# A feed-forward product whose moving operand and whose sums are walked backwards in time

## The chip, the core and the metric

The kernel runs on one core of a Trainium2 chip. The metric is the device time of one execution in microseconds (us), the median over several runs. A smaller time is better. A core has a matrix engine (PE in the profile: matmuls; PEld: the loads of its weights), a vector engine (DVE), an activation engine (ACT), a general engine (POOL), and a queue for transfers (SP). PE reads its operands from the on-chip memory and writes its sums to a separate accumulator memory, PSUM, in banks of 128 rows by 512 fp32 numbers.

## The reference, cut to what matters

The whole block is a token mixing (two attention branches, gates, an output projection, a layer norm) and then a gated feed-forward. The change touches only the first product of the feed-forward, `x @ w_ffn_in`.

```python
x = layer_norm(DEEPNORM_ALPHA * x + merged @ w_out[layer], ln1_g[layer], ln1_b[layer])
u, g = jnp.split(x @ w_ffn_in[layer], 2, axis=-1)
h = jax.nn.gelu(causal_dwconv(u, conv_w[layer], conv_b[layer])) * g
x = layer_norm(DEEPNORM_ALPHA * x + h @ w_ffn_out[layer], ln2_g[layer], ln2_b[layer])
```

There are 512 frames, 1024 channels, and 2816 hidden channels for each of `u` and `g`. All numbers are fp32.

## The kernel before

The feed-forward works on transposed data: channels lie on the 128 rows of the memory, and frames run along each row. After the first layer norm the tile `x1h` holds the 8 blocks of 128 channels by 512 frames, rounded to the short fp32 format that PE takes, and `x1l` holds what the rounding left over. Every weight piece comes the same way, as a rounded part (`whi`) and a rest (`wlo`), which ACT (L104) and DVE (L113) make from what a transfer brought.

`ffn_in` (L932 to L939) computes one block of 128 hidden channels for a range of frames `c`. It runs over the 8 blocks of input channels, and for each issues three products into the same PSUM bank: rounded by rounded (L937), weight by rest (L938), weight's rest by rounded (L939). So one block takes 24 products that add up in place. The weights are the stationary operand; the frames are the moving operand, which is streamed column by column, and column t of the sum lands in column t of the bank.

The call sites are in the main body. The first three blocks (`u0`, `g0`, `u1`) are done in two halves of 256 frames, `t_lo` and `t_hi` (L1036 to L1041), because the last quarter of the frames is turned between them. All other blocks take the 512 frames at once (`full`): `g1` at L1044, and then in the loop over f from 2 to 21 `u{f}` at L1059 and `g{f}` at L1074. Together these are 44 blocks: 41 of 24 products with 512 frames, and 3 of 48 products with 256.

When the bank of `u` is full, ACT copies it to a padded tile (L980), DVE runs the causal convolution of width 3 over it (L982 to L984), ACT applies the GELU (L985), and DVE multiplies it with the bank of `g` (L993). Between the blocks PE also issues the products of the feed-forward's second matrix that are ready (`first_products`, L1024 to L1029, through `product`, L1013 to L1019). For f = 2 these open two new banks P0 and P1.

The order of the instructions on each engine is fixed when the program is built; at run time an engine takes its instructions in that order and waits on semaphores. PSUM has two banks for `u` and `g` in the loop, so the reader of a bank has the length of a block or more to empty it.

Of the kernel before, what the change touches and what calls it, by code (L numbers as in the profile page):

```python
# [23 lines left out]
KC = D // 128  # L24
# [103 lines left out]
def tile_block(ctx: ExitStack, tc: tile.TileContext, xT, xN, w_qi, w_ki, w_t, w_v, w_br, w_o, w_fi, w_fo,  # L128
               bg, cw, rel, onehot, lnp, out):
    nc = tc.nc  # L130
# [25 lines left out]
    def pa(name):  # L156
        return psA.tile([128, 512], F32, tag="A", name=name)

    def pb(name):
        return psB.tile([128, 512], F32, tag="B", name=name)  # L160
# [47 lines left out]
    ps = pb("idle_ps")  # L208
# [91 lines left out]
    for k in range(KC):  # L300
# [8 lines left out]
        wh, wl = st.get(f"qi{k}")  # L309
        for n in range(4):  # L310
            c = slice(n * 128, n * 128 + 128)
# [360 lines left out]
    for a, b in ((0, 512), (512, NREL)):  # L672
        ps = pa("line_ps")
# [134 lines left out]
    for p in range(4):  # L808
        wh_wl = st.get(f"ba{p}")
        for n in (2 * p, 2 * p + 1):  # L810
            if n not in early and n not in gps:
                gps[n] = whole(proj_t(f"ga{n}"))
            ps = pb("ba_ps")
            wh, wl = wh_wl
            for k in range(4):
                c = slice((n % 2) * 512 + k * 128, (n % 2) * 512 + k * 128 + 128)
# [39 lines left out]
    x1h = qp.tile([128, KC, S], F32R, name="x1h")  # L856
    x1l = qp.tile([128, KC, S], F32R, name="x1l")
# [74 lines left out]

    def ffn_in(w, ps, c):
        wh, wl = w
        for k in range(KC):
            kc = slice(k * 128, k * 128 + 128)
            nc.tensor.matmul(ps[:, c], wh[:, kc], x1h[:, k, c], start=(k == 0), stop=False)  # L937
            nc.tensor.matmul(ps[:, c], wh[:, kc], x1l[:, k, c], start=False, stop=False)  # L938
            nc.tensor.matmul(ps[:, c], wl[:, kc], x1h[:, k, c], start=False, stop=(k == KC - 1))  # L939

# [93 lines left out]
    for w, ps in zip(w0, ps0):  # L1036
        if ps is ps0[2]:
            turn(NB - 1)
        ffn_in(w, ps, t_lo)
    for w, ps in zip(w0, ps0):  # L1040
        ffn_in(w, ps, t_hi)  # L1041
    activate(0, ps0[0], ps0[1])
    g1_ps = pa("g_ps")
    ffn_in(st.get("g1"), g1_ps, full)  # L1044
    activate(1, ps0[2], g1_ps)
    close(ac)
# [252 lines left out]
```

## Time and profile before

| what | value |
|---|---|
| time, median of 3 runs | 746.79 us (746.69 to 747.53) |
| span of the profiled execution, first to last instruction | 744.9 us |
| the profiled execution's own time | not listed apart from the three runs; they lie 1.8 to 2.6 us above its span |
| PE busy | 735.6 us, 99% of the span |
| DVE, ACT, POOL busy | 572.0, 408.0, 148.8 us |
| PE's granted clock | 0.998 of full speed over the span |

The profile is one execution, recorded instruction by instruction. A row of a timeline gives the start in us, the length in us, the engine, the line of the kernel, the operation with its tiles (output, then inputs), and the shape. The length of a matmul runs from its first column to its modelled end, and the next one starts before that end, so the price of a matmul in a dense run is the distance from start to start and not its length.

### The profile page before, as it was taken

What the parts mean: (1) busy time and instruction counts of PE and PEld (TensorE: products, weight loads), DVE (VectorE), ACT (ScalarE), POOL (GpSimd) and SP (SyncE); (2) the same over time, 40 slices, a digit from 0 to 9 for tenths busy, and PEclk for the clock granted to TensorE, in tenths of its full rate; (3) what the DMA queues carried; (4) which work ended last, traced back from release to release, by engine and by line L of the source; (5) the groups of instructions that cost most, each with busy time, mean ns of one, the idle gap of its engine ahead of it and who ended that gap; (6) DMA issues with size and microseconds to landing.
All of it is one profiled execution on the core that took longest, in us unless ns stands there. A gap on an engine that the chain in (4) does not pass through costs nothing.

```text
span 744.9 us, 9755 instructions
## 1 busy us (share of the span) xinstructions
PE 735.6 (99%) x3477; PEld 616.9 (83%) x3477; DVE 572.0 (77%) x907; ACT 408.0 (55%) x572; POOL 148.8 (20%) x161
## 2 busy tenths in 40 slices
PE   9999999999999999999999999999999999999995
PEld 7888888888888888888889888888888888888885
DVE  5569888999679898668755866686767668668985
ACT  6466867797785587845473533443444344345430
POOL 0002224365743332000101111011101101110011
PEclk9999999999999999999999999999999999999999
DMA  7445887796476455527832544444443444448632
GB/s 266 157 128 188 207 172 173 158 214 163 116 181 154 135 126 136 131 85 247 289 57 86 170 141 142 141 143 143 141 166 114 161 136 149 144 140 268 202 130 84
DMA packets 73631, 117.03 MB, mean 157 GB/s; under 512 B 42536, under 2 KB 42792, under 8 KB 73584
## 3 DMA queue, kind: packets, MB, share of 16 engines
q1 hardware_dynamic: 66304, 93.98, 42.0%
q0 software_dynamic: 5744, 18.38, 9.9%
q10 hardware_dynamic: 1536, 4.06, 2.1%
q8 instruction: 27, 0.44, 0.3%
q14 instruction: 20, 0.16, 0.1%
HBM read 95.93 MB, written 9.98 MB: 142 GB/s over the span
## 4 chain that ended last, share of the span: by engine, by line
PE 89%; DVE 3%; POOL 2%; issue 2%; DMA 2%; ACT 2%; DVEq 0%; POOLq 0%; ACTq 0%
PE u_ps L937 5%; PE u_ps L939 5%; PE g_ps L937 5%; PE u_ps L938 5%; PE g_ps L939 5%; PE g_ps L938 5%; PE m L1019 2%; PE m L1017 2%; PE m L1018 2%; PE av_ps L511 2%; PE ga_ps L234 2%; PE ga_ps L233 2%; PE gb_ps L235 2%; PE gb_ps L234 2%; PE ga_ps L235 2%; PE gb_ps L233 2%
## 5 line engine op out<-in xcount | busy, mean ns | idle before, releaser
L104 ACT ACTIVATE whi<-raw 128x1024 fp32r<-128x1024 f32 (+1 forms) x124 | 123.8, 1001 | 143.1 <-PE g_ps L938 43.7
L113 DVE TENSOR_TENSOR wlo<-raw,whi 128x1024 fp32r<-128x1024 f32 (+1 forms) x105 | 123.9, 1181 | 36.3 <-ACT whi L104 35.6
L939 PE MATMUL u_ps<-x1h,wlo 128*128 128x512 f32 (+1 forms) x192 | 71.4, 372 | 0.0
L937 PE MATMUL u_ps<-x1h,whi 128*128 128x512 f32 (+1 forms) x192 | 71.3, 372 | 0.0
L938 PE MATMUL u_ps<-x1l,whi 128*128 128x512 f32 (+1 forms) x192 | 71.3, 371 | 0.0
L937 PE MATMUL g_ps<-x1h,whi 128*128 128x512 f32 (+1 forms) x184 | 69.9, 380 | 0.0
L938 PE MATMUL g_ps<-x1l,whi 128*128 128x512 f32 (+1 forms) x184 | 69.9, 380 | 0.0
L939 PE MATMUL g_ps<-x1h,wlo 128*128 128x512 f32 (+1 forms) x184 | 69.9, 380 | 0.0
L939 PEld LDWEIGHTS u_ps<-x1h,wlo 128*128 128x128 f32 x192 | 36.2, 188 | 6.3
L938 PEld LDWEIGHTS u_ps<-x1l,whi 128*128 128x128 f32 x192 | 36.2, 188 | 6.3
L937 PEld LDWEIGHTS u_ps<-x1h,whi 128*128 128x128 f32 x192 | 36.2, 188 | 6.2
L939 PEld LDWEIGHTS g_ps<-x1h,wlo 128*128 128x128 f32 x184 | 34.6, 188 | 6.6
L938 PEld LDWEIGHTS g_ps<-x1l,whi 128*128 128x128 f32 x184 | 34.6, 188 | 6.5
L937 PEld LDWEIGHTS g_ps<-x1h,whi 128*128 128x128 f32 x184 | 34.6, 188 | 6.5
L960 DVE TENSOR_TENSOR t<-raw 128x512 f32<-128x512 f32 x11 | 7.6, 693 | 40.1 <-DMA raw<-in_w_fo_dram 39.2
L569 POOL TENSOR_TENSOR bm<-win,score 128x256 f32<-128x256 f32 (+2 forms) x24 | 26.9, 1147 | 32.2 <-DMA pl<-bm 27.3
L985 ACT ACTIVATE c<-c,cwt 128x512 f32<-128x512 f32 x22 | 15.9, 725 | 27.5 <-DVE c L984 27.3
L979 POOL MEMSET u<- 128x2 f32 x22 | 2.1, 98 | 143.7 <-ACT whi L104 99.2
L993 DVE TENSOR_TENSOR hF<-g_ps,c 128x512 f32<-128x512 f32 x22 | 15.1, 687 | 19.7 <-PE g_ps L939 19.7
L835 POOL TENSOR_TENSOR rstd<-rstd,mhalf 128x1 f32<-128x1 f32 x8 | 7.7, 959 | 104.6 <-DVE rstd L834 104.6
L423 DVE MAX8 m<-score 128x8 f32<-128x256 f32 (+2 forms) x48 | 26.6, 556 | 0.9
L557 POOL TENSOR_TENSOR beta<-beta,keep 128x1280 f32<-128x1280 f32 x8 | 21.6, 2704 | 26.7 <-DVE keep L554 26.7
(576 smaller groups left out, 2088.3 us busy)
## 6 DMA issues: line engine op xcount, KB each, us to landing
raw<-in_w_fi_dram SPq DMA_DIRECT2D x44, 512.0 KB, 3.3
raw<-in_w_t_dram SPq DMA_DIRECT2D x32, 512.0 KB, 3.7
raw<-in_w_fo_dram SPq DMA_DIRECT2D x26, 512.0 KB, 4.2
wlo<-in_w_t_dram POOLq DMA_DIRECT2D x14, 512.0 KB, 5.8
raw<-in_w_br_dram SPq DMA_DIRECT2D x8, 512.0 KB, 4.0
raw<-in_w_o_dram SPq DMA_DIRECT2D x8, 512.0 KB, 4.1
raw<-in_w_v_dram SPq DMA_DIRECT2D x7, 512.0 KB, 4.6
raw_b<-in_w_fo_dram SPq DMA_DIRECT2D x6, 512.0 KB, 5.5
```

What stands on the lines that cost most here:

```text
L104: self.high = nc.scalar.activation(hi[:, :w], t[:, :w], AF.Copy).ins
L113: self.done[key] = eng.tensor_sub(lo[:, :w], t[:, :w], r32(hi[:, :w])).ins
L233: nc.tensor.matmul(ps[:M], wh[:, c], xh[k], start=(k == 0), stop=False)
L234: nc.tensor.matmul(ps[:M], wh[:, c], xl[k], start=False, stop=False)
L235: nc.tensor.matmul(ps[:M], wl[:, c], xh[k], start=False, stop=(k == KC - 1))
L423: nc.vector.max(m8, sc)
L557: nc.gpsimd.tensor_mul(beta, beta, keep[:, 1:ATT + 1])
L569: nc.gpsimd.tensor_add(bm[:, OFF[j]:OFF[j] + N], win[:, 512 - N:512], score[j])
L937: nc.tensor.matmul(ps[:, c], wh[:, kc], x1h[:, k, c], start=(k == 0), stop=False)
L938: nc.tensor.matmul(ps[:, c], wh[:, kc], x1l[:, k, c], start=False, stop=False)
L939: nc.tensor.matmul(ps[:, c], wl[:, kc], x1h[:, k, c], start=False, stop=(k == KC - 1))
L985: nc.scalar.activation(c, c, AF.Gelu_apprx_tanh, bias=cwt[:, f, 3:4])
```

## The change

Both the moving operand and the output of the three products get a step of -1 along the frames. The last frame of the range is streamed first, and its sum goes to the last column of the range, so that column t of the bank still holds frame t.

```diff
     def ffn_in(w, ps, c):
         wh, wl = w
+        dst = ps[:, c][:, ::-1]
         for k in range(KC):
             kc = slice(k * 128, k * 128 + 128)
-            nc.tensor.matmul(ps[:, c], wh[:, kc], x1h[:, k, c], start=(k == 0), stop=False)
-            nc.tensor.matmul(ps[:, c], wh[:, kc], x1l[:, k, c], start=False, stop=False)
-            nc.tensor.matmul(ps[:, c], wl[:, kc], x1h[:, k, c], start=False, stop=(k == KC - 1))
+            xkh, xkl = x1h[:, k, c][:, ::-1], x1l[:, k, c][:, ::-1]
+            nc.tensor.matmul(dst, wh[:, kc], xkh, start=(k == 0), stop=False)
+            nc.tensor.matmul(dst, wh[:, kc], xkl, start=False, stop=False)
+            nc.tensor.matmul(dst, wl[:, kc], xkh, start=False, stop=(k == KC - 1))
```

Two lines are added, so L937, L938 and L939 become L939, L940 and L941, and everything behind them moves down by two. In the built program every one of these products has a step of -1 and starts at the last element of its range, on the read side and on the write side. The stationary operand is as before. No instruction stands elsewhere on any engine, and the waits are the same but for one: the first product into bank P1 (for f = 2) now also waits for a semaphore of PE itself, at the count which the last product of `g1` sets. PE gets one more instruction for it, a bare semaphore wait, since a product carries one wait.

## The prediction

> **What bounds the kernel now.** I read the page's head and its first part, then the chain that ended last, then PE's waits, to learn whether a longer matmul could hide anywhere.
>
> ```profile
> span 744.9 us, 9755 instructions
> ...
> PE 735.6 (99%) x3477; PEld 616.9 (83%) x3477; DVE 572.0 (77%) x907; ACT 408.0 (55%) x572; POOL 148.8 (20%) x161
> ...
> PE 89%; DVE 3%; POOL 2%; issue 2%; DMA 2%; ACT 2%; DVEq 0%; POOLq 0%; ACTq 0%
> ```
>
> PE is busy for 735.6 of 744.9 us, and 89% of the chain that ended last is PE. A busy PE need not be at its peak, so the next view is who PE waited for; its columns are the total wait, the number of waits and the longest, in us.
>
> ```profile
> PE idle_ps L210 <- DVE idle L207: 1.2, 1, 1.2
> PE bs_ps L613 <- DVE wlo L113: 0.3, 1, 0.3
> PE qi_ps L312 <- ACT whi L104: 0.3, 1, 0.3
> ```
>
> These three are all, and none is in the feed-forward. Then the busy time by stretches: the half-width blocks (390.6 to 407), the full blocks (407 to 673), and the tail.
>
> ```profile
> 390.60:407.00 16.40, 16.40 (x138) 16.36 (x137) 8.67 (x14) 6.49 (x8) 2.18 (x5) 1.00 0.22 66
> 407.00:673.00 266.00, 266.00 (x1183) 220.60 (x1182) 191.10 (x253) 109.76 (x138) 35.91 (x53) 1.00 0.44 147
> 673.00:744.90 71.90, 64.38 (x315) 54.40 (x313) 58.39 (x87) 24.86 (x28) 6.02 (x8) 0.97 0.51 169
> ```
>
> The columns are the stretch and its length, then PE, PEld, DVE, ACT and POOL busy, the granted clock, and transfers. In the feed-forward's main stretch PE has no gap at all (266.00 of 266.00) at the full clock, while DVE is busy for 191.10 and ACT for 109.76. So the first product sits on the path with every nanosecond, and the others have room: **whatever one product gains or loses goes into the time in full**.
>
> How much of the span do the touched products hold? Their groups, of one shape each (busy us, mean ns of one, idle before), and two pairs from the timeline:
>
> ```profile
> L937 PE MATMUL g_ps<-x1h,whi 128*128 128x512 f32 x168 | 65.4, 389 | 0.0
> L937 PE MATMUL u_ps<-x1h,whi 128*128 128x512 f32 x160 | 62.2, 389 | 0.0
> ...
> L937 PE MATMUL u_ps<-x1h,whi 128*128 128x256 f32 x32 | 9.1, 285 | 0.0
> ...
> L937 PE MATMUL g_ps<-x1h,whi 128*128 128x256 f32 x16 | 4.5, 283 | 0.0
> ```
> ```profile
> 559.92 0.39 PE L937 MATMUL u_ps<-x1h,whi 128*128 128x512 f32 x1
> ...
> 565.36 0.39 PE L937 MATMUL g_ps<-x1h,whi 128*128 128x512 f32 x1
> ```
> ```profile
> 407.74 0.28 PE L939 MATMUL u_ps<-x1h,wlo 128*128 128x256 f32 x1
> ...
> 408.94 0.40 PE L937 MATMUL g_ps<-x1h,whi 128*128 128x512 f32 x1
> ```
>
> L938 and L939 have the same counts as L937, so there are 3 x (168 + 160) = 984 products of 512 frames and 3 x (32 + 16) = 144 of 256. From 559.92 to 565.36 stand 24 products, one every 226.7 ns; from 407.74 to 408.94 stand 10 of the narrow ones, one every 120 ns. Together 984 x 0.2267 + 144 x 0.120 = 223.1 + 17.3 = **240.4 us**, a third of the span. The two distances give the price of a frame as well: (226.7 - 120) / 256 = 0.417 ns, and a fixed part of 226.7 - 512 x 0.417 = 13.3 ns.
>
> **The change, part by part.** It moves no instruction, removes none, and adds one bare wait. There are three terms: the price of a frame when the stream runs backwards, the fixed part of a product, and the wait.
>
> *The frame.* 984 x 512 + 144 x 256 = 540,672 frames are streamed at 0.417 ns. No matmul of this profile has a step of -1, so the price is bounded by the nearest rows. On the low side stand matmuls whose moving operand is not one run: the attention's weighted sum reads 384 columns as three runs of 128 that lie 384 apart, beside 384 adjacent columns in the indexer's product.
>
> ```profile
> L314 PE MATMUL qi_ps<-xh,wlo 128*128 128x384 f32 x32 | 9.4, 335 | 0.0
> ...
> L511 PE MATMUL av_ps<-ptl,va 128*128 128x384 f32 x16 | 5.4, 336 | 0.0
> ```
>
> 336 against 335 ns: leaving a run costs nothing that can be seen. But these are two hops in 384 columns on the read side alone, and the sums go to adjacent columns in both. On the high side stands the only work here that steps by -1, a running product on DVE that reads two operands and writes one backwards (L554), against DVE's forward work on two operands (means over 11 of each).
>
> ```profile
> 80.98 1.21 DVE L554 TENSOR_TENSOR_SCAN keep<-keep,first 128x512 f32<-128x512 f32 x1
> ...
> 83.98 0.67 DVE L554 TENSOR_TENSOR_SCAN keep<-keep,first 128x256 f32<-128x256 f32 x1
> ```
> ```profile
> L962 DVE TENSOR_TENSOR raw<-raw,raw 128x512 f32<-128x512 f32 x11 | 7.5, 682 | 0.1
> ...
> L1000 DVE TENSOR_TENSOR hF<-hF 128x256 f32<-128x256 f32 x11 | 4.6, 419 | 0.0
> ```
>
> Backwards, an element costs (1.21 - 0.67) / 256 = 2.1 ns; forwards (682 - 419) / 256 = 1.03 ns. The factor of two may be the direction, or that each element of a running product needs the one before it; these rows can't part the two. I take it as the upper bound: one frame in two clocks, 0.833 ns, so 540,672 x 0.417 = +225 us. Below nothing I see no room: each frame must still pass, and 0.42 ns is also what lies between L314's 384 columns and L937's 512, (389 - 335) / 128. Between ends so far apart I take the matmul rows, since they are of the same engine and show that it forms an address for each column and isn't held to one ascending run: **0 us**. The step has the same size as before, and two frames that follow each other are still neighbours, on both sides. The upper end is kept for the range.
>
> *The fixed part.* 13.3 ns of each product aren't streaming. The first address is the far end of the same row. If turning cost as much again it would be 1128 x 13.3 = +15 us, and if all of it went, -15 us; nothing in the change touches it, and I take 0.
>
> *The wait.* The first product into P1 now waits for the end of the last product of `g1`, and a bare semaphore instruction comes before it. In the trace before:
>
> ```profile
> 414.18 0.39 PE L939 MATMUL g_ps<-x1h,wlo 128*128 128x512 f32 x1
> ...
> 420.52 0.39 PE L1017 MATMUL P<-whi,ah 128*128 128x512 f32 x1
> ```
>
> The one ends at 414.57, the other starts at 420.52: the condition has held for 6 us when it is asked. What such an instruction costs is seen where PE already has one, in the same stage:
>
> ```profile
> L937 PEldq EVENT_SEMAPHORE  x1: 51/51/51, 663.3 to 663.3; - x1
> ```
> ```profile
> 663.06 0.39 PE L939 MATMUL u_ps<-x1h,wlo 128*128 128x512 f32 x1
> 663.28 0.39 PE L937 MATMUL u_ps<-x1h,whi 128*128 128x512 f32 x1
> 663.51 0.39 PE L938 MATMUL u_ps<-x1l,whi 128*128 128x512 f32 x1
> ```
>
> It takes 51 ns in PE's sequencer, and the products around it keep their distance (0.22, 0.23 us), since the sequencer is ahead of the array. So 0; without that cover, 0.05 us. Behind it on PE stands all of the feed-forward, but 0.05 us once is nothing here.
>
> *The readers.* Column t of a bank still holds frame t, and ACT's copy and DVE's product wait for the last of the 24 products as before. They see no difference. If PE were slower they would only wait longer.
>
> **The sum.** 744.9 + 0 + 0 + 0 = 744.9 us of span. The three timed runs lie 1.8 to 2.6 us above the profiled span, their median 1.9 us; with that the forecast is **746.8 us**, the median of before.
>
> **The rivals.** *One frame in two clocks (slower).* PE takes 0.417 ns a frame, the fastest rate it shows. If that rate needs two frames to be fetched or stored as one ascending pair, a step of -1 splits each pair. It decides as soon as either side, the read or the sums, has this condition. 540,672 x 0.417 = +225 us gives 972 us, or 957 us if the 13.3 ns then hide behind the slower stream (512 x 0.833 = 427 instead of 226.7 ns: 984 x 0.200 + 144 x 0.093 = 210). For it speaks the factor of two on DVE; against it the runs of L511, which only bear on reading.
> [...]
>
> *A part of it.* Say one clock is lost in every fourth frame: 540,672 / 4 x 0.417 = +56 us, 803 us. No row has such a price; it stands for all that lies between 762 and 957.
>
> *A price at the turn.* Up to 13.3 ns more for each product, at most +15 us: up to 762 us. Against it: the L511 products start at many places of their rows and show no such thing.
>
> *The change doesn't do what it says.* Were the direction dropped on the way to the chip, the time would be that of the forecast, but the built instructions hold the step of -1, so this is no case of its own.
>
> **How the numbers follow.** No cost 0.62; a price at the turn 0.06; a part 0.06; one frame in two clocks 0.22; worse than that 0.03; a gain from the fixed part 0.01. The forecast's own range is 745.5 to 748.2 us, 0.2% to either side (about what a measurement of this kernel can tell from no change). That holds only 0.62, and turn and part together raise it to 0.74, so a range that holds 8 in 10 must reach the two-clock case: 745.5 to 975 us. Faster 0.01, within 0.2% 0.62, slower 0.37.
>
> **What would show it.** In the profile after, one product of 512 frames should start every 227 ns and one of 256 every 120 ns. A distance near 427 to 440 ns and 213 to 227 ns is the two-clock rival; the same surplus on both widths is a price at the turn; a surplus in the ratio of the widths is a price of the frame. P1's first product should follow P0's last by 0.23 us. If PE's distances stay and the time still moves, my reading that nothing else changes is wrong. The forecast fails if the chip pairs frames by an ascending step rather than by where they lie.

## The result, and the profile after

The changed kernel takes 754.29 us (median of 4 runs, 753.66 to 754.48) against 747.16 us before in the same comparison: a ratio of 1.0095, 95% interval 1.008 to 1.011. It is slower by 7.1 us. The head of the page, its first part and the chain by engine:

```profile
span 752.3 us, 9756 instructions
...
PE 742.8 (99%) x3477; PEld 617.1 (82%) x3477; DVE 571.8 (76%) x907; ACT 408.7 (54%) x572; POOL 149.5 (20%) x161
...
PE 89%; DVE 4%; POOL 2%; issue 2%; ACT 1%; DMA 1%; SPq 0%; DVEq 0%; POOLq 0%; ACTq 0%
```

PE is busy for 7.2 us more; the other engines' busy times are within 1 us of what they were. By stretches (length, then busy time of PE, PEld, DVE, ACT, POOL, granted clock, transfers), cut where the same work begins and ends:

```profile
407.80:680.70 272.90, 272.90 (x1184) 221.00 (x1183) 191.12 (x253) 110.02 (x138) 35.84 (x53) 1.00 0.43 143
680.70:752.30 71.60, 64.13 (x314) 54.20 (x312) 58.40 (x87) 24.54 (x27) 6.03 (x8) 0.97 0.49 169
```

The full blocks again leave PE no gap and the clock is full, but they last 272.9 us for the same work (to one product at the cut) instead of 266.0. So each product takes longer. Two pairs from the timeline, 24 products of 512 frames apart and 15 of 256 apart:

```profile
559.51 0.40 PE L939 MATMUL g_ps<-x1h,whi 128*128 128x512 f32 x1
...
565.11 0.40 PE L939 MATMUL u_ps<-x1h,whi 128*128 128x512 f32 x1
```
```profile
407.83 0.28 PE L939 MATMUL u_ps<-x1h,whi 128*128 128x256 f32 x1
...
409.61 0.40 PE L939 MATMUL g_ps<-x1h,whi 128*128 128x512 f32 x1
```

A product of 512 frames starts every 5.60 / 24 = **233.3 ns instead of 226.7**; one of 256 frames every 1.78 / 15 = **118.7 ns instead of 120**. Summed over all start-to-start distances of the touched products, the 984 wide ones take 229.6 us after 223.1 (+6.6), the 144 narrow ones 17.2 after 17.4 (-0.2). Products that stand between them take 0.2 us more. That is 6.6 of the 7.4 us of span. The rest, 0.9 us, lies ahead of the feed-forward, whose first product starts at 391.7 instead of 390.8 us. Most of it is there long before a changed product runs: a bare wait of PE that starts at 28.55 us before starts at 29.28 after. In the traces of the full kernels below, that wait starts anywhere from 28.61 to 29.15 and the feed-forward from 390.5 to 391.1, whatever the direction. So 0.9 us is not in the touched products; that it would vanish in other executions of the changed kernel is not shown.

PE's waits (total, number, longest) show no wait in the feed-forward, and the added wait on P1 does what the forecast said:

```profile
PE idle_ps L210 <- DVE idle L207: 1.2, 1, 1.2
PE vs_ps L270 <- ACT whi L104: 0.6, 1, 0.6
PE l_ps L580 <- POOL qa2a L359: 0.2, 1, 0.2
```
```profile
421.28 0.39 PE L1021 MATMUL P<-whi,al 128*128 128x512 f32 x1
421.51 0.39 PE L1019 MATMUL P<-whi,ah 128*128 128x512 f32 x1
```

The second row is the product that waits: 0.23 us behind the last product into P0.

### The profile page after: what moved, and what is told of

It is laid out like the page before. It is cut to its first block, busy times and chain, and to the rows that moved or that the text cites. A ratio compares the mean times of both kernels' runs of the same rounds, so it can differ in the third digit from the quotient of the medians.

```text
span 752.3 us, 9756 instructions
## 1 busy us (share of the span) xinstructions
PE 742.8 (99%) x3477; PEld 617.1 (82%) x3477; DVE 571.8 (76%) x907; ACT 408.7 (54%) x572; POOL 149.5 (20%) x161
## 4 chain that ended last, share of the span: by engine, by line
PE 89%; DVE 4%; POOL 2%; issue 2%; ACT 1%; DMA 1%; SPq 0%; DVEq 0%; POOLq 0%; ACTq 0%
PE g_ps L940 5%; PE u_ps L940 5%; PE u_ps L939 5%; PE g_ps L939 5%; PE u_ps L941 5%; PE g_ps L941 5%; PE m L1020 2%; PE m L1021 2%; PE m L1019 2%; PE av_ps L511 2%; PE gb_ps L235 2%; PE ga_ps L234 2%; PE ga_ps L233 2%; PE gb_ps L233 2%; PE ga_ps L235 2%
## 5 line engine op out<-in xcount | busy, mean ns | idle before, releaser
L941 PE MATMUL u_ps<-x1h,wlo 128*128 128x512 f32 (+1 forms) x192 | 72.7, 379 | 0.0
L939 PE MATMUL u_ps<-x1h,whi 128*128 128x512 f32 (+1 forms) x192 | 72.6, 378 | 0.0
L940 PE MATMUL u_ps<-x1l,whi 128*128 128x512 f32 (+1 forms) x192 | 72.6, 378 | 0.0
L940 PE MATMUL g_ps<-x1l,whi 128*128 128x512 f32 (+1 forms) x184 | 71.3, 388 | 0.0
L939 PE MATMUL g_ps<-x1h,whi 128*128 128x512 f32 (+1 forms) x184 | 71.3, 387 | 0.0
L941 PE MATMUL g_ps<-x1h,wlo 128*128 128x512 f32 (+1 forms) x184 | 71.2, 387 | 0.0
L940 PEld LDWEIGHTS u_ps<-x1l,whi 128*128 128x128 f32 x192 | 36.1, 188 | 7.4
L939 PEld LDWEIGHTS u_ps<-x1h,whi 128*128 128x128 f32 x192 | 36.1, 188 | 7.2
L941 PEld LDWEIGHTS u_ps<-x1h,wlo 128*128 128x128 f32 x192 | 36.1, 188 | 7.2
L941 PEld LDWEIGHTS g_ps<-x1h,wlo 128*128 128x128 f32 x184 | 34.6, 188 | 7.6
L940 PEld LDWEIGHTS g_ps<-x1l,whi 128*128 128x128 f32 x184 | 34.6, 188 | 7.6
L939 PEld LDWEIGHTS g_ps<-x1h,whi 128*128 128x128 f32 x184 | 34.6, 188 | 7.5
```

What stands on the lines that cost most here:

```text
L939: nc.tensor.matmul(dst, wh[:, kc], xkh, start=(k == 0), stop=False)
L940: nc.tensor.matmul(dst, wh[:, kc], xkl, start=False, stop=False)
L941: nc.tensor.matmul(dst, wl[:, kc], xkh, start=False, stop=(k == KC - 1))
```

## The experiments

### Which side costs it: the read or the sums

In the first kernel only the moving operand runs backwards, in the second only the sums.

```diff
-        dst = ps[:, c][:, ::-1]
+        dst = ps[:, c]
```

```diff
-            xkh, xkl = x1h[:, k, c][:, ::-1], x1l[:, k, c][:, ::-1]
+            xkh, xkl = x1h[:, k, c], x1l[:, k, c]
```

> The changed kernel with the step of -1 on the moving operand alone; the sums go forwards, so that a bank holds the frames in reverse and the output is that of reversed frames. Theory 1 (the backwards sums cost the 6.7 ns a product): 512-frame products start every 227 ns again and the time is that of before, 747 us. Theory 2 (the backwards read costs it): 233 ns, 754 us. Theory 3 (it takes both, each hides the other or adds half): something between, about 750 us.

> The changed kernel with the step of -1 on the sums alone; frames are read forwards, so that a bank holds them in reverse and the output is that of reversed frames. Theory 1 (the backwards sums cost it): 512-frame products every 233 ns and about 754 us. Theory 2 (the backwards read costs it): 227 ns, 747 us. Theory 3: about 750 us.

Backwards read alone: 753.25 us, ratio 1.0081 (1.0065 to 1.0098). Backwards sums alone: 746.92 us, ratio 0.9997 (0.9988 to 1.0006). The timelines, 24 products apart, first of the read and then of the sums:

```profile
559.62 0.40 PE L939 MATMUL g_ps<-x1h,whi 128*128 128x512 f32 x1
...
565.22 0.40 PE L939 MATMUL u_ps<-x1h,whi 128*128 128x512 f32 x1
```
```profile
559.75 0.39 PE L939 MATMUL u_ps<-x1h,whi 128*128 128x512 f32 x1
...
565.19 0.39 PE L939 MATMUL g_ps<-x1h,whi 128*128 128x512 f32 x1
```

5.60 us against 5.44 us. Summed as above, the wide products take 229.6 us with the backwards read alone, as in the changed kernel, and 223.1 us with the backwards sums alone, as before; the narrow ones take 17.2 and 17.4. In the products, then, **the read carries all of it**, and a step of -1 on the sums is free. The medians (6.3 us more against 7.1) agree within their intervals.

### What kind of price it is: widths, directions, bfloat16

A kernel of nothing but groups of 48 products in the same form (24 into one bank, three to a block of weights), one group for each width and direction. The core of it, here for backwards read and sums at width N:

```python
for n in range(24):
    k, w, x = n // 3, (wh, wh, wl)[n % 3], (xh, xl, xh)[n % 3]
    nc.tensor.matmul(rev(ps[:, 0:N]), w[:, k * 128:k * 128 + 128], rev(x[:, k, 0:N]), start=(n == 0), stop=(n == 23))
```

> No part of the block is computed; the output is a copy of the input. Groups of 48 products in the form of the feed-forward's first product, one group for each width (512, 448, 384, 256, 128) and each of four directions (read and sums forwards or backwards), then groups in which the direction changes from product to product, groups of 510 frames, the upper 256 frames, and bfloat16. Forwards every width should take 13.3 ns and 0.417 ns a frame. If a backwards frame costs more (by 6.7/512 = 0.013 ns), 448, 384 and 256 should cost 5.8, 5.0 and 3.3 ns more than forwards; if it is a price at the turn, 6.7 ns more at every width; if it takes a whole row or bank of 512 to be walked, only 512 costs more, and 510 and the upper 256 frames say whether the end of the row matters. The trace after has 256 backwards at 118.3 ns against 120 ns, which neither of the first two gives. If the price is one of the weights' load meeting the stream, bfloat16, whose weights load faster, should show none.

Each of these small kernels was executed once. Here and below, a figure for a group is the mean of its start-to-start distances from the seventh product on, where they have settled. The very first group here starts slowly (its first distances are 427 ns and more), so the forwards figure at 512 frames is that of the group whose sums alone run backwards. First and last product of two groups of 512 frames (sums alone backwards, then read alone backwards) and of two of 256 (forwards, then both backwards):

```profile
31.24 0.39 PE L62 MATMUL a_fr<-xh,wh 128*128 128x512 f32 x1
...
41.89 0.39 PE L62 MATMUL a_fr<-xh,wl 128*128 128x512 f32 x1
42.12 0.40 PE L68 MATMUL a_rf<-xh,wh 128*128 128x512 f32 x1
...
53.09 0.40 PE L68 MATMUL a_rf<-xh,wl 128*128 128x512 f32 x1
```
```profile
137.55 0.28 PE L128 MATMUL d_ff<-xh,wh 128*128 128x256 f32 x1
...
143.18 0.28 PE L128 MATMUL d_ff<-xh,wl 128*128 128x256 f32 x1
...
154.75 0.28 PE L146 MATMUL d_rr<-xh,wh 128*128 128x256 f32 x1
...
160.30 0.28 PE L146 MATMUL d_rr<-xh,wl 128*128 128x256 f32 x1
```

Over all 47 distances, (41.89 - 31.24) / 47 = 226.6 and (53.09 - 42.12) / 47 = 233.4 ns; at 256 frames 5.63 / 47 = 119.8 and 5.55 / 47 = 118.1. The small kernel repeats what the large one does, at 512 frames to a tenth of a nanosecond, and again the sums' direction changes nothing at any width (0.1 ns at most).

| frames | 128 | 256 | 384 | 448 | 512 | 512, bfloat16 |
|---|---|---|---|---|---|---|
| read forwards, ns | 111.7 | 120.0 | 173.3 | 202.7 | 226.7 | 215.8 |
| read backwards, ns | 111.6 | 118.3 | 177.8 | 206.8 | 233.3 | 215.8 |

The surplus is nothing at 128 frames, then -1.7, +4.5, +4.1 and +6.7 ns. It is neither one number (a price at the turn) nor even in the frames (a price of a frame), and it is not there at 512 alone (a whole row): these theories miss. 510 frames from the start of the row cost 233.3 backwards like 512, so it isn't the row's last frames; 510 frames that begin 8 bytes later cost 235.6. In bfloat16, where all three products of a block had the same operands, there is no surplus, as the theory of the weights' load had it; the groups' rows (start, length of all 47 that were recorded):

```profile
238.05 10.53 PE L212 MATMUL bf_ff<-xb,wb 128*128 128x512 bf16 x47
248.42 10.52 PE L218 MATMUL bf_rr<-xb,wb 128*128 128x512 bf16 x47
```

With the direction changing from product to product the distance is 230.0 ns, the mean of both; changing after every three, 233.4, which the mean of two fixed prices does not give.

### Is it the weights' load

An fp32 load takes 188 ns in the records and a bfloat16 one 97, so the load meeting the stream was the next theory. Fewer weight columns, and the weights moved along their rows, in outline:

```diff
-    nc.tensor.matmul(rev(ps[:, 0:N]), w[:, k * 128:k * 128 + 128], ...
+    nc.tensor.matmul(rev(ps[0:M, 0:N]), w[:, off + k * 128:off + k * 128 + M], ...
```

> No part of the block is computed; the output is a copy of the input. Groups of 48 products of 512 frames (some of 256 or 448), each forwards and backwards. The widths' run showed fp32 products of 512 frames at 226.7 ns forwards and 233.3 backwards, bfloat16 ones at 215.8 both ways, and widths that no single price of a frame fits. Theory A: the surplus over 215.8 is the weights' load meeting the frames' read, since an fp32 load takes 188 ns against 97; then fewer weight columns (96, 64, 32) shorten the load and shrink the surplus in both directions and the gap between them, roughly in proportion (gap 6.7, 5, 3.3, 1.7 ns); and moving the weights against the frames by 8 to 512 bytes changes the backwards price, since it changes which addresses meet. Theory B: the surplus belongs to the fp32 stream itself (a restart at the end of a row); then the gap stays 6.7 ns whatever the weights' columns or place are, and at 256 frames backwards stays 1.7 ns below forwards.

| weight columns (512 frames) | 128 | 96 | 64 | 32 |
|---|---|---|---|---|
| forwards, ns | 226.7 | 230.0 | 229.9 | 231.7 |
| backwards, ns | 233.3 | 233.3 | 233.3 | 233.3 |

At 512 frames theory A falls: the load shrinks from 188 to 109 ns, and nothing gets cheaper. At 256 frames it does, forwards above all. The first and last product of the forwards group of 256 frames with 64 columns:

```profile
119.39 0.28 PE L119 MATMUL Hc_f<-xh,wh 128*64 128x256 f32 x1
...
124.73 0.28 PE L119 MATMUL Hc_f<-xh,wl 128*64 128x256 f32 x1
```

(124.73 - 119.39) / 47 = 113.6 ns, settled 113.3 instead of 120.0; backwards fell only from 118.3 to 117.7, so that here the reversal costs 4.4 ns instead of gaining 1.7. The load does count, then, but not in proportion to its length. Theory B, a gap that stays, falls too. At 512 frames forwards got dearer, and with the weights moved by 16, 32 or 64 bytes it took 233.3, 233.3 and 233.4 ns, as much as backwards. At 256 bytes both were at their old values. At 128 bytes backwards took 240.0. At 448 frames, with frames and sums moved by 16 to 256 bytes, forwards took 200.0 to 204.0 ns and backwards stayed at 206.6 to 206.7. So it matters where weights and frames lie, and the next run went through all places.

> No part of the block is computed; the output is a copy of the input. Groups of 48 products of 512 frames, forwards and backwards, with the weights moved by 0 to 248 bytes in steps of 8, and then with 2, 8 and 16 weight columns. The run before fell against a price in proportion to the load: with 32 of 128 columns a product still took 231.7 forwards and 233.3 ns backwards, but moving the weights by 64 bytes made forwards 233.4 and by 128 bytes made backwards 240. Theory A2 (the price is set by which addresses the load and the stream meet at): the groups repeat after 256 bytes, forwards is 226.7 ns at some places only and as dear as backwards at others, and with 2 columns, whose load is all but nothing, both directions fall to about 216 ns. Theory B2 (backwards has a floor of its own): no place of the weights brings backwards below 233 ns, and 2 columns leave it at 233 ns.

| 32 places, 0 to 248 bytes in steps of 8 | lowest | mean | highest | at the lowest |
|---|---|---|---|---|
| forwards, ns | 226.7 | 231.8 | 234.3 | 3 places (0, 120, 216 bytes) |
| backwards, ns | 233.3 | 233.7 | 236.6 | 28 places |

Each theory was half right. The place decides for forwards (A2): only 3 of 32 places give 226.7. Backwards has a floor of 233.3 (B2) that none of these places goes under. The forwards group with the weights moved by 224 bytes, and then the backwards group with two weight columns, which is still at the floor; first and last product of each:

```profile
656.66 0.39 PE L455 MATMUL Wfg_f<-xh,wh 128*128 128x512 f32 x1
...
667.63 0.39 PE L455 MATMUL Wfg_f<-xh,wl 128*128 128x512 f32 x1
```

```profile
757.17 0.40 PE L518 MATMUL Mac_r<-xh,wh 128*2 128x512 f32 x1
...
768.14 0.40 PE L518 MATMUL Mac_r<-xh,wl 128*2 128x512 f32 x1
```

(667.63 - 656.66) / 47 = 233.4 ns forwards with the full load, and (768.14 - 757.17) / 47 = 233.4 ns backwards with a load of 83 ns, which A2 had taken as all but nothing. Forwards takes 231.1, 226.7 and 231.1 ns with 2, 8 and 16 columns: at 512 frames it is not how long the load lasts. The place at 128 bytes gave 236.6 backwards here and 240.0 in the run before, so that place has more than one steady value.

### The place, in the kernel itself

If the kernel of before stands at one of the good places, moving the frames must cost it what the reversal costs, with no step of -1 anywhere. `x1h` and `x1l` become one tile that begins 8 numbers (32 bytes) later; a third kernel begins 64 numbers (256 bytes) later, as the control.

```diff
-    x1h = qp.tile([128, KC, S], F32R, name="x1h")
-    x1l = qp.tile([128, KC, S], F32R, name="x1l")
+    xx = qp.tile([128, 2 * KC * S + 64], F32R, name="x1hl")[:, 8:8 + 2 * KC * S].rearrange("p (n k t) -> p n k t", n=2, k=KC)
+    x1h, x1l = xx[:, 0], xx[:, 1]
```

> The kernel of before, frames read forwards, with x1h and x1l both 32 bytes further along their rows (one tile that begins 8 numbers later); instructions, order and waits are those of before. The offsets' run showed forwards at 226.7 ns only where weights and frames lie together in a few ways, the place of this kernel among them, and at 233.4 ns with the weights 224 bytes further, which is the frames 32 bytes further; backwards stayed at 233.3 there. Theory A3 (the kernel of before stands at a favourable place, which the backwards read can't use): 512-frame products every 233 ns, and the time that of the changed kernel, 753 to 755 us, with no backwards step in it. Theory B3 (the direction alone sets it): 227 ns and 747 us.

> The changed kernel, read and sums backwards, with x1h and x1l both 32 bytes further along their rows. Theory A3: backwards is the same at nearly every place, so 233 ns and 753 to 755 us again, and the difference between the two directions is gone. Theory B3: 754 us here too, but 747 us in the forwards kernel beside it.

> The forwards kernel with x1h and x1l in one tile as in the 32-byte shift, but 256 bytes further along the row instead of 32. It parts the shift from the joining of the two tiles. Theory A3 (the place sets it, with a period of 256 bytes): 227 ns and 747 us. If the joint tile or its size had made the 32-byte kernel slow: 233 ns and 753 us here too.

| kernel | time, us | ratio to before (95%) | 512 frames, ns |
|---|---|---|---|
| before | 747.0 | | 226.7 |
| forwards, 32 bytes on | 753.14 | 1.0084 (1.0069 to 1.0099) | 233.3 |
| backwards, 32 bytes on | 753.49 | 1.0087 (1.0070 to 1.0104) | 233.3 |
| forwards, 256 bytes on | 746.99 | 1.0000 (0.9990 to 1.0010) | 226.7 |

The forwards kernel 32 bytes on, the backwards one 32 bytes on, then the forwards one 256 bytes on, each 24 products apart:

```profile
559.60 0.40 PE L937 MATMUL g_ps<-x1hl,whi 128*128 128x512 f32 x1
...
565.20 0.40 PE L937 MATMUL u_ps<-x1hl,whi 128*128 128x512 f32 x1
```
```profile
559.54 0.40 PE L939 MATMUL g_ps<-x1hl,whi 128*128 128x512 f32 x1
...
565.14 0.40 PE L939 MATMUL u_ps<-x1hl,whi 128*128 128x512 f32 x1
```
```profile
559.32 0.39 PE L937 MATMUL u_ps<-x1hl,whi 128*128 128x512 f32 x1
...
564.76 0.39 PE L937 MATMUL g_ps<-x1hl,whi 128*128 128x512 f32 x1
```

5.60, 5.60 and 5.44 us. **Thirty-two bytes cost a wide product what the reversal costs it**, at that place the two directions are alike, and the control shows that it is the place and not the joint tile. The narrow products move the other way here too: the 144 of them take 17.0 us forwards instead of 17.4.

### More widths, and the frames moved

> No part of the block is computed; the output is a copy of the input. Groups of 48 products, forwards and backwards, at widths from 160 to 512 frames, and at 512 frames with the frames moved along their rows by 8 to 256 bytes (2 to 64 numbers). Theory A3: moving the frames does what moving the weights did: 226.7 ns forwards at few places, 229 to 234 at most, backwards 233.3 or more at all, and 256 bytes give the start again. The distances so far are multiples of 6.67 ns (120.0, 173.3, 200.0, 226.7, 233.3, 240.0), or their mean over two to five products is; so at every width backwards and forwards should differ by whole or shared steps of 6.67 ns, with no constant price of a frame. A price of a frame would grow evenly with the width, a price at the turn would be one number.

| frames | 288 | 320 | 352 | 416 | 480 |
|---|---|---|---|---|---|
| forwards, ns | 131.7 | 146.7 | 160.0 | 186.7 | 216.7 |
| backwards, ns | 133.3 | 146.7 | 162.2 | 191.1 | 220.0 |

At 160, 192 and 224 frames both directions take 111.6 to 111.8 ns; at 496 it is 223.3 and 226.7, at 504 it is 226.8 and 228.9. Moved by 256 bytes the groups are at 226.7 and 233.3 again. At the ten smaller shifts forwards took 228.9 to 234.2, at eight of them 232.4 or more, and backwards 233.3 to 235.6. Moving the frames changes the price as moving the weights does. Many steady fp32 distances sit on a grid of 6.67 ns (120.0, 146.7, 160.0, 220.0, 226.7, 233.3, 240.0 are 18, 22, 24, 33, 34, 35 and 36 steps). One step is the time of 16 frames (16 x 0.417, the estimate from the distances of before), so by that estimate widths that are multiples of 16 stream for a whole number of steps anyway; but 510 frames, which are not, also cost 35 steps backwards. Others would fit as a sum over two to five products (118.3 is 71 / 4 steps, 177.8 is 80 / 3), which is weak evidence, since almost any number comes near some such sum. At 512 frames and the place of the kernel of before, the reversal is one step of this grid.

## Why the prediction came out as it did

The forecast, no change at 746.8 us with 745.5 to 748.2 around it, missed: the kernel takes 754.29 us. That lies in the stated range, 745.5 to 975 us, only because the range had been stretched to a rival, one frame in two clocks, that did not come true. So the range held by luck.

*Where the time would go.* Right. The first product is on the path with every nanosecond: 6.4 us more in the touched products and 0.2 us in those between them, against 7.1 us in the median (6.0 to 8.2 by the interval). No engine hid or added anything that the runs could tell from the scatter.

*One frame in two clocks.* Rightly set below the forecast. Neither the read nor the sums halve their rate: a product of 512 frames starts every 233.3 ns with the read backwards and every 226.7 ns with the sums backwards (kernel ratio 0.9997), where this rival had 427 to 440 ns. That frames are fetched or stored in pairs, which it supposed, no run shows.

*The price of a frame, taken as 0.* Right in kind: the surplus does not grow evenly with the frames (-1.7, +4.5, +4.1 and +6.7 ns at 256, 384, 448 and 512). That PE forms an address for each column, named beside it, was the author's reading of the 335 and 336 ns of L314 and L511; no run shows it.

*The fixed part, taken as 0 because "nothing in the change touches it".* **This is the step that failed.** 13.3 ns was read from two rows as a constant of a product. The runs show that at 512 frames it is the least of many values. It depends on where weights and frames lie within a stretch of 256 bytes (read forwards, a product of 512 frames takes 233.3 ns with the frames moved by 32 bytes, and 226.7 again with them moved by 256) and on the read's direction (233.3 ns backwards at the place of before). By the estimate of 0.417 ns a frame, a product of 512 frames read backwards has 20.0 ns beside its streaming (233.3 - 213.3), one of 256 frames 11.6 (118.3 - 106.7). The bound of 15 us to either side held; the change cost 984 x 6.67 ns = 6.6 us of it and gave 0.2 us back on the narrow products.

*A price at the turn.* This rival named the size, up to 762 us, and had a chance of 0.06. Its mechanism is not what the runs show: the narrow products of this kernel gain (118.7 ns after 120), and the same price comes without any turn when the frames move by 32 bytes (233.3 ns). The L511 rows, taken as evidence that start places don't matter, could not show it. They were lengths of matmuls and not distances from start to start, and the frames of every L511 product start at a multiple of 128 numbers (512 bytes) in their tile: by the 256 bytes found here, all at the same place.

*The wait, the readers.* Right: P1's first product follows 0.23 us behind its predecessor, and no wait appears in the feed-forward.

What stays open is why. That the fp32 stream and its weights meet in a pattern locked to steps of 6.67 ns is the author's guess from the distances; what the steps are, and why a backwards read of 512 frames reaches no better place than 35 of them, no run here shows. Nor do they show why a shorter load helps 256 frames (113.3 ns with 64 weight columns instead of 120.0) and not 512 (229.9 instead of 226.7). A stream of fp32 frames without any load before it, and weights that are read backwards too, were not tried.

## What to carry to other kernels

Where matmuls run back to back as here, a few nanoseconds more for each of a thousand products are a per cent of the kernel (984 x 6.67 ns = 6.6 of 747 us); a product's price should be read as a distance from start to start, and treated as a property of this layout, not of the instruction. After any edit that moves an operand in memory or changes how it is read, look at that distance first: here 32 bytes were worth 6.1 us, nearly as much as the whole change. A backwards output costs nothing here (746.92 us, ratio 0.9997), so where a kernel like this one needs a reversal, the write is the side to try first.

## What the runs showed of the hardware that was not expected

Fp32 products of 512 frames took 226.7 to 240.0 ns for the same work, in kernels whose granted clock was 0.985 to 0.998 over the span, by the place of their operands within 256 bytes and the direction of the read; in bfloat16 at the one place that was tried it was 215.8 ns in both directions. Even the good fp32 place of the kernel of before is 10.9 ns a product above that, and none of the places tried came under 226.7. Forwards, 3 of 32 places reached it; backwards, none went under 233.3.
